# Empty bytes ahead of the tiles that TensorE streams: moving FFN and attention tiles to another byte address

## The chip, the cores and the metric

The kernel runs on one core of a Trainium2 chip. The metric is the device time of one execution in microseconds, the median of several runs. No instruction does other arithmetic after the change than before; what changes is where tiles stand in the core's SBUF (the on-chip memory, 128 partitions wide; an address here is a byte within each partition).

## The reference, cut to what matters

Two layers over 256 latent and 256 context tokens, width 1024, each layer an attention between two SwiGLU FFNs of inner width 2816; layer 0 has differential attention, layer 1 grouped-query attention.

```python
def swiglu(h, w_in, w_out):
    gate, up = jnp.split(h @ w_in, 2, axis=-1)
    return (jax.nn.silu(gate) * up) @ w_out
...
x = x + 0.5 * mod[:, 2] * swiglu(modulate(x, norm_g[i, 0], mod[:, 0], mod[:, 1]), w_ffn_in[i, 0], w_ffn_out[i, 0])
h = modulate(x, norm_g[i, 1], mod[:, 3], mod[:, 4])
y, yc = diff_attention(h, hc, ...)  # layer 0; gqa_attention in layer 1
x = x + mod[:, 5] * y
x = x + 0.5 * mod[:, 8] * swiglu(modulate(x, norm_g[i, 2], mod[:, 6], mod[:, 7]), w_ffn_in[i, 1], w_ffn_out[i, 1])
```

The context stream has the same products with the same weights, up to the last layer, whose last FFN has latent tokens alone.

## The kernel before, in words

**Products.** Activations lie transposed: 128 features on the partitions, the 512 tokens (256 latent, then 256 context) along the free bytes. Every float32 number is split into a rounded part and the rest, `hi` and `lo`, and one product is three matmuls (helper `mac`, lines 384 to 386): `hi` by `hi`, `hi` by the other's `lo`, `lo` by the other's `hi`. The weight, 128 by 128, is held in the array; the activation, 128 by 512 (or 256, or 258), streams past it. Each matmul has its own load of the held tile (PEld), which runs while the matmul before it streams. So while one activation tile streams, the next weight is read too.

**Stages.** In an FFN, half of the inner width at a time (`NH` = 11 tiles): first products `gate` and `up` stream `h_hi`, `h_lo` (24 matmuls each); `gated` makes `a_hi`, `a_lo` of them; the second products `out` stream `a_hi`, `a_lo` (33 matmuls for each of 8 tiles of features). The last two feature tiles of an FFN are done a stream at a time, 256 columns wide, under the name `e`, in `boundary`. The last FFN has 258 (first products) and 256 columns (second products). In the attentions, `qk`, `q`, `k` and `v` stream `h` (in `v` the weight streams and `h` is held), the scores `sps` hold `qs` and stream `ks` and `kl`, and the output projection (`op`) streams `pa`; its second half in layer 0, under the name `e`, streams the first four tiles of `h_hi` and `h_lo`, in which those parts are kept.

**Weights.** `advance` issues each weight's DMA on SP's queue into one of 5 `raw` slots; ScalarE rounds it into one of 6 `whi` slots (line 150), VectorE subtracts into one of 6 `wlo` slots (line 151). The same `raw` slots take the modulation weights (`wm`), which VectorE multiplies and sums (`mod_task`, line 172) between its other work, in program order.

**Where tiles stand.** A pool is laid out when it is opened, tile behind tile in the order in which they are first asked for, each rounded up to 32 bytes, and pools opened later stand behind it. The pools `const`, `wpool`, `stat` and `tmp` stay open for the whole kernel; the FFN's, `da`'s or `gq`'s pool stands behind them, at byte 151072, one after the other in the same place. This gives, with the remainder of the address by 512:

| tiles | part in a product | bytes | remainder before | after |
|---|---|---|---|---|
| `whi`, `wlo` (all 12 slots) | held (in `v` streamed) | 56992 to 106143 | 160 | 160 |
| `hhi0..7`, `hlo0..7` | streamed (in `v` held) | 109728 to 142495 | 160 | 160 |
| `ahi0..10`, `alo0..10` | streamed | from 151072 | 32 | 160 |
| `da`: `kl` / `pa` | streamed | from 151136 | 96 / 96 | 160 / 160 |
| `da`: `ks` / `qs` / `v` | streamed / held / streamed | from 175968 | 352 | 160 |
| `da`: `pe` / `pT` | held | from 213920 | 416 / 160 | 224 / 480 |
| `gq`: `qs`, `ks`, `kl`, `pa`, `v`, `pe` | both | from 151072 | 32 | 160 |
| `gq`: `pT0`, `pT1` | streamed | from 210848 | 416 | 32 |

A tile of 512 float32 columns has 2048 bytes, a held tile 512 bytes, and a weight slot is cut into held tiles at multiples of 512 bytes, so one remainder stands for a whole tile.

Of the kernel before, what the change touches and what calls it, by code (L numbers as in the profile page):

```python
# [11 lines left out]
F32 = mybir.dt.float32  # L12
F32R = mybir.dt.float32r
# [6 lines left out]
P = 128  # L20
D = 1024
KD = D // P
SEQ = 256
CTX = 256
T = SEQ + CTX
# [18 lines left out]
PIECE_AT = (18, 21, 24, 26, 28, 31, 32, 33)  # L44
WARM = 24


@with_exitstack
def trunk(ctx: ExitStack, tc: tile.TileContext, a: dict):
    nc = tc.nc  # L50
    PSUM = bass.MemoryType.PSUM

    const = ctx.enter_context(tc.tile_pool(name="const", bufs=1))
    wpool = ctx.enter_context(tc.tile_pool(name="wpool", bufs=2))
    stat = ctx.enter_context(tc.tile_pool(name="stat", bufs=1))
    tmp = ctx.enter_context(tc.tile_pool(name="tmp", bufs=3))
# [6 lines left out]
    def ax_tile(name):  # L63
        return ax_ps.tile([P, 512], F32, tag="ax", name=name)


    tok = (slice(0, SEQ), slice(SEQ, T))

    sck = tmp.tile([P, KD, 32], F32, tag="sq", name="sck")
# [65 lines left out]
    def raw_tile(name):  # L135
        return wpool.tile([P, 1024], F32, tag="raw", name=name, bufs=5)

    def advance(upto):
        for i in range(len(ready), min(upto, len(flat) - 1) + 1):
            src, pieces, f = flat[i]  # L140
            parts, c0 = [], 0
            for q, kt in enumerate(pieces):
                n = kt * f
                raw = raw_tile(f"raw{i}_{q}")
                nc.sync.dma_start(raw[:, :n], src[:, c0 : c0 + n])
                hi = wpool.tile([P, 1024], F32R, tag="whi", name=f"whi{i}_{q}", bufs=6)
                lo = wpool.tile([P, 1024], F32R, tag="wlo", name=f"wlo{i}_{q}", bufs=6)
                step = n // 2 if i in fine else n
                for c in (slice(b, b + step) for b in range(0, n, step)):
                    nc.scalar.activation(hi[:, c], raw[:, c], AF.Copy)  # L150
                    nc.vector.tensor_tensor(lo[:, c], raw[:, c], hi[:, c].bitcast(F32), op=ALU.subtract)  # L151
                parts += [(hi[:, k * f : k * f + f], lo[:, k * f : k * f + f]) for k in range(kt)]
                c0 += n
            ready[i] = parts

    def weight(i, look=LOOK):
        advance(i + look)
        return ready[i]
# [165 lines left out]
    def table(func, after):  # L324

        t = tmp.tile([P, 1], F32, tag="tab", name="tab")
        return nc.scalar.activation(t, after, func, scale=0.0, bias=1.0)

    h_hi = [stat.tile([P, T], F32R, name=f"hhi{j}", tag=f"hhi{j}") for j in range(KD)]
    h_lo = [stat.tile([P, T], F32R, name=f"hlo{j}", tag=f"hlo{j}") for j in range(KD)]  # L330

    def modulated_tile(l, n3, s, j, rstd, eng=nc.vector):
# [98 lines left out]
    def boundary(groups, nxt, follow):  # L431


        for s in range(2):
            for i, (outs, ends, tiles) in enumerate(groups):
                ps = [mm_tile(f"e{t}") if t < 3 and not (s and i) else ax_tile(f"e{t}") for t in range(tiles)]
                outs(ps, tok[s])
                if s and i == len(groups) - 1:
                    advance(nxt)
                ends(ps, s)  # L440
            if s:
                advance(nxt + 1)
            steps.extend(modulated(*follow, s))
            if s == 0:
                norm_step()
                norm_step()


    def ffn(l, s, n, follow=None, f_steps=0, o_steps=0, upto=(0, 0)):
# [4 lines left out]
        nxt = base  # L454
        with ExitStack() as st:
            fp = st.enter_context(tc.tile_pool(name=f"ffn{l}{s}", bufs=2))
            a_hi = [fp.tile([P, T], F32R, tag=f"ahi{i}", name=f"ahi{i}", bufs=1) for i in range(NH)]
            a_lo = [fp.tile([P, T], F32R, tag=f"alo{i}", name=f"alo{i}", bufs=1) for i in range(NH)]

            def load_sc(after=None):  # L460
# [33 lines left out]
            for hf in range(2):  # L494
                i0 = 0
                if hf == 0 and opening:
                    i0 = G0
                    with tc.tile_pool(name="open", bufs=2) as sp:
# [7 lines left out]
                        for k in range(KD + 2):  # L506
# [8 lines left out]
                            if k > 1:  # L515
                                w = ready[nxt + k - 2]
# [12 lines left out]
                elif hf == 0:  # L529
                    i0 = 2  # L530
                    banks = [mm_tile(f"g{b}") if b < 3 else ax_tile(f"g{b}") for b in range(4)]
                    w = [weight(nxt, 1), weight(nxt + 1, 0)]
# [15 lines left out]
                for i in range(i0, NH):  # L548
                    w = weight(nxt)
# [9 lines left out]
                for jj in range(0, KD, 2):  # L559
# [18 lines left out]
                    w = [weight(nxt), weight(nxt + 1, 0 if final else LOOK)]  # L578
# [97 lines left out]
    def diff_attention(l):  # L676
        base = start["att", l]
        scale = 64 ** -0.5
        with tc.tile_pool(name="da", bufs=2) as ap:
            lam = ap.tile([P, 4], F32, tag="lam", name="lam", bufs=1)  # L680
            nlam = lam[:, 3:4]
            g1 = ap.tile([P, 1], F32, tag="g1", name="g1", bufs=1)

            lamv = tmp.tile([P, 4, 64], F32, tag="ht", name="lamv")
            for i, n in enumerate(("da_lam_q1", "da_lam_k1", "da_lam_q2", "da_lam_k2")):
                nc.scalar.dma_start(lamv[:, i, :], a[n].to_broadcast([P, 64]))

            kls = [[ap.tile([P, T], F32R, tag=f"kl{i}{m}", name=f"kl{i}{m}", bufs=1) for m in range(2)] for i in range(2)]
            for kl in kls:
                zero_others(kl)  # L690

            def lambdas(after):
                lj = ap.tile([P, 64], F32, tag="lj", name="lj", bufs=1)
                for i in range(2):
                    nc.vector.tensor_tensor_reduce(
                        out=lj, in0=lamv[:, 2 * i, :], in1=lamv[:, 2 * i + 1, :], op0=ALU.mult, op1=ALU.add,
                        scale=1.0, scalar=0.0, accum_out=lam[:, i : i + 1],
                    )
                table(AF.Exp, after)
                nc.scalar.activation(lam[:, 0:2], lam[:, 0:2], AF.Exp)  # L700
                nc.vector.tensor_tensor(lam[:, 2:3], lam[:, 1:2], lam[:, 0:1], op=ALU.subtract)
                nc.vector.tensor_scalar(nlam, lam[:, 2:3], -LAM_INIT, None, op0=ALU.add)
                nc.vector.tensor_scalar(g1, subln_g, 1.0 - LAM_INIT, None, op0=ALU.mult)

            pa = [[ap.tile([P, T], F32R, tag=f"pa{i}{k}", name=f"pa{i}{k}", bufs=1) for k in range(4)] for i in range(2)]

            def v_mac(ps, w, k, s_, t):
                c = slice(s_ * 256 + t * P, s_ * 256 + t * P + P)
# [58 lines left out]
            def outputs(hd):  # L767
                ops = ax_tile("ops")
                h = hd["h"]
                for u in range(4):  # L770
                    k0 = 0 if u < 2 else 2
                    for kt in range(k0, 4):
                        nc.tensor.matmul(
                            ops[:, u * P : u * P + P], hd["pT"][u][:, kt - k0, :],
                            hd["v"][:, kt, (h % 2) * P : (h % 2) * P + P], start=kt == k0, stop=kt == 3,
                        )
                o, ms = hd["o"], hd["ms"]
                nc.vector.tensor_copy(o[:, :, h % 2, :], ops.rearrange("p (t f) -> p t f", t=4))
                for u in range(4):
                    osq = ap.tile([P, P], F32, tag="osq", name="osq", bufs=1)  # L780
                    nc.scalar.activation(
                        osq, ops[:, u * P : u * P + P], AF.Square, accum_out=ms[:, u, h % 2 : h % 2 + 1]
                    )
# [26 lines left out]
            def behind(hd, u):  # L810

                turned(hd, u)
                if u == U_AT and done:
                    pair = done.pop()
                    scaled(pair)
                    h = pair["h"]
                    if h < HEADS // 2:
                        parts_of(pair, o_hi[h - 1 : h + 1], o_lo[h - 1 : h + 1])
                    else:
                        late.append(pair)  # L820
                if u == 3:
                    outputs(hd)
                    if hd["h"] % 2:
                        normed(hd)
                        done.append(hd)
# [44 lines left out]
            for s_ in range(2):  # L870
# [5 lines left out]
                for k in range(KD):  # L876
                    for g in range(2):
                        mac(
                            qkps[g][:, tok[s_]], w_part(wqk, k, slice(g * P, g * P + P)), h_part(k, tok[s_]),
                            k == 0, k == KD - 1,  # L880
                        )
            lambdas(last_norm["rstd"][:, 0:1])
            v_tile(0)
            for t in range(2):
# [27 lines left out]
    def gqa(l):  # L912
        base = start["att", l]
        scale = 64 ** -0.5
        with tc.tile_pool(name="gq", bufs=2) as ap:
            qs = [ap.tile([P, SEQ], F32R, tag=f"qs{i % 8}", name=f"qs{i}", bufs=1) for i in range(16)]
            ks = [ap.tile([P, T], F32R, tag=f"ks{i}", name=f"ks{i}", bufs=1) for i in range(4)]
            kl = [ap.tile([P, T], F32R, tag=f"kl{i}", name=f"kl{i}", bufs=1) for i in range(4)]
# [3 lines left out]
            pa = [[ap.tile([P, SEQ], F32R, tag=f"pa{i}{k}", name=f"pa{i}{k}", bufs=1) for k in range(8)] for i in range(2)]  # L922
# [136 lines left out]
            for n, un in enumerate(units + [None, None]):  # L1059
                if un:  # L1060
                    flight.append((un, weights_of(*un)))
                if n in Q_AT:
                    i, g = divmod(Q_AT.index(n), 2)
# [8 lines left out]
                if n in sqs:  # L1072
                    i, sq = sqs[n]
# [11 lines left out]
            out_proj(base + 8, range(4, 8), o_part, l, SEQ, 1, (l, 2))  # L1085

    ffn(0, 0, T, (0, 1), 2, 1, (0, 7))
    diff_attention(0)
    ffn(0, 1, T, (1, 0), 1.5, 1, (1, 1))
    ffn(1, 0, T, (1, 1), 1.5, 1, (1, 8))  # L1090
    gqa(1)
    ffn(1, 1, SEQ)

# [102 lines left out]
```

## Time and profile before

| | |
|---|---|
| median of 3 runs | 1728.6 us (1728.1 to 1730.68) |
| the profiled execution's own time | 1729.97 us |
| its span, first to last instruction | 1727.8 us |
| TensorE (PE) busy | 1707.0 us, 9586 matmuls |
| VectorE (DVE) / ScalarE (ACT) busy | 1159.4 / 730.3 us |
| granted clock, mean | 0.996 |

A matmul's length in the rows runs from its start to its modelled end, and neighbours overlap; what a matmul costs the engine is the distance from its start to the next one's start, here called its pace. It is read from the time order of a stretch without waits: the start of the last row less that of the first, by the number of steps between them.

### The profile page before, as it was taken

Reading aid. Unit: us, or ns where it says so; the run is one execution under the profiler, and the core shown is the slowest. Engines: PE = TensorE matmul, PEld = TensorE weight load, DVE = VectorE, ACT = ScalarE, POOL = GpSimd, SP = SyncE. Lnnn points to the kernel's source line nnn. Section 1 sums busy time; section 2 is a strip of 40 time slices with the busy share of each in tenths; the row PEclk is TensorE's granted clock in tenths of the full one; section 3 lists DMA queues with packets and bytes.
Section 4 is the critical chain, followed back from the end, with each engine's and each line's share of the span. In section 5 each row is a group of like instructions: output and inputs, shape, how many; then the busy total and the mean of one; then the engine's idle time right before and its main releaser. Section 6 shows DMA issues by size and latency. Waiting matters only on the chain.

```text
span 1727.8 us, 24899 instructions
## 1 busy us (share of the span) xinstructions
PE 1707.0 (99%) x9586; PEld 1463.1 (85%) x9586; DVE 1159.4 (67%) x2113; ACT 730.3 (42%) x1359; POOL 26.3 (2%) x42
## 2 busy tenths in 40 slices
PE   9999999999999999999999999999999999999998
PEld 6788888789888889888888898888888897799998
DVE  3697777756888868756766557545543488876664
ACT  3432222235767646322222244222222368765454
POOL 0000000000100000000000000000000010000000
PEclk8999999999999999999999999999999999999999
DMA  7675565442122223545644535546552332145652
GB/s 255 228 242 160 187 215 161 153 151 101 57 67 74 73 74 123 179 140 160 203 156 150 169 110 183 152 132 196 178 160 77 118 101 72 50 164 146 217 162 83
DMA packets 76870, 249.59 MB, mean 144 GB/s; under 512 B 9936, under 2 KB 10064, under 8 KB 76752
## 3 DMA queue, kind: packets, MB, share of 16 engines
q1 hardware_dynamic: 75456, 247.25, 44.9%
q8 instruction: 75, 1.23, 0.3%
q10 hardware_dynamic: 1296, 0.76, 0.1%
q14 instruction: 43, 0.35, 0.1%
HBM read 246.92 MB, written 1.05 MB: 144 GB/s over the span
## 4 chain that ended last, share of the span: by engine, by line
PE 84%; DVE 7%; issue 3%; DMA 2%; ACT 2%; POOL 0%; DVEq 0%; ACTq 0%; POOLq 0%
PE out L385 7%; PE out L386 7%; PE out L384 7%; PE gate L384 7%; PE gate L385 7%; PE gate L386 7%; PE up L385 7%; PE up L386 7%; PE up L384 7%; DMA wm<-in_w_mod 2%; PE g L384 2%; PE g L385 2%; PE g L386 2%; DVE junk L172 1%; PE e L384 1%
## 5 line engine op out<-in xcount | busy, mean ns | idle before, releaser
L150 ACT ACTIVATE whi<-raw 128x1024 fp32r<-128x1024 f32 (+3 forms) x426 | 350.4, 836 | 455.7 <-PE out L385 248.5
L151 DVE TENSOR_TENSOR wlo<-raw,whi 128x1024 fp32r<-128x1024 f32 (+3 forms) x426 | 399.6, 946 | 186.5 <-ACT whi L150 185.7
L172 DVE CUSTOM_DVE_ANT_0 junk<-wm,sc,b_mod 128x1024 bf16<-128x1024 f32 x224 | 287.4, 1283 | 186.4 <-DMA wm<-in_w_mod 182.8
L384 PE MATMUL gate<-hhi,whi 128*128 128x512 f32 (+1 forms) x648 | 234.0, 361 | 0.7 <-DVE av L474 0.7
L386 PE MATMUL gate<-hhi,wlo 128*128 128x512 f32 (+1 forms) x648 | 233.7, 361 | 0.0
L385 PE MATMUL gate<-hlo,whi 128*128 128x512 f32 (+1 forms) x648 | 233.6, 361 | 0.0
L385 PE MATMUL up<-hlo,whi 128*128 128x512 f32 (+1 forms) x648 | 233.6, 361 | 0.0
L384 PE MATMUL up<-hhi,whi 128*128 128x512 f32 (+1 forms) x648 | 233.6, 360 | 0.0
L386 PE MATMUL up<-hhi,wlo 128*128 128x512 f32 (+1 forms) x648 | 233.5, 360 | 0.0
L385 PE MATMUL out<-alo,whi 128*128 128x512 f32 (+1 forms) x638 | 232.3, 364 | 0.0
L384 PE MATMUL out<-ahi,whi 128*128 128x512 f32 (+1 forms) x638 | 232.0, 364 | 0.0
L386 PE MATMUL out<-ahi,wlo 128*128 128x512 f32 (+1 forms) x638 | 231.8, 364 | 0.0
L402 ACT ACTIVATE ahi<-av 128x512 fp32r<-128x512 f32 (+1 forms) x88 | 50.7, 578 | 211.8 <-DVE av L474 204.5
L384 PEld LDWEIGHTS gate<-hhi,whi 128*128 128x128 f32 x648 | 122.4, 189 | 20.2 <-DVE av L474 1.6
L385 PEld LDWEIGHTS out<-alo,whi 128*128 128x128 f32 x638 | 119.9, 188 | 21.4 <-DVE alo L403 0.4
L386 PEld LDWEIGHTS gate<-hhi,wlo 128*128 128x128 f32 x648 | 122.4, 189 | 18.4
L385 PEld LDWEIGHTS up<-hlo,whi 128*128 128x128 f32 x648 | 122.4, 189 | 18.4
L384 PEld LDWEIGHTS up<-hhi,whi 128*128 128x128 f32 x648 | 122.4, 189 | 18.4
L386 PEld LDWEIGHTS up<-hhi,wlo 128*128 128x128 f32 x648 | 122.4, 189 | 18.3
L385 PEld LDWEIGHTS gate<-hlo,whi 128*128 128x128 f32 x648 | 122.4, 189 | 18.2
L386 PEld LDWEIGHTS out<-ahi,wlo 128*128 128x128 f32 x638 | 119.7, 188 | 21.1
L384 PEld LDWEIGHTS out<-ahi,whi 128*128 128x128 f32 x638 | 119.8, 188 | 21.0
(240 smaller groups left out, 2618.0 us busy)
## 6 DMA issues: line engine op xcount, KB each, us to landing
raw<-in_w_in SPq DMA_DIRECT2D x170, 512.0 KB, 4.4
wm<-in_w_mod SPq DMA_DIRECT2D x128, 512.0 KB, 4.2
raw<-in_w_out SPq DMA_DIRECT2D x64, 384.0 KB, 3.4
raw<-in_w_out SPq DMA_DIRECT2D x64, 320.0 KB, 3.1
raw<-in_da_vqk SPq DMA_DIRECT2D x24, 512.0 KB, 3.9
wf<-in_w_mod SPq DMA_DIRECT2D x16, 512.0 KB, 5.0
raw<-in_gq_qkv SPq DMA_DIRECT2D x12, 512.0 KB, 3.8
raw<-in_da_o SPq DMA_DIRECT2D x8, 512.0 KB, 3.7
```

Of the source, the lines that this page charges most:

```text
L150: nc.scalar.activation(hi[:, c], raw[:, c], AF.Copy)
L151: nc.vector.tensor_tensor(lo[:, c], raw[:, c], hi[:, c].bitcast(F32), op=ALU.subtract)
L172: nc.vector.tensor_tensor_reduce(out=junk, in0=raw, in1=mod_pool["sc"][:, s, :], op0=ALU.mult, op1=ALU.add, scale=1.0, scalar=b_mod[:, l, ...
L384: nc.tensor.matmul(out, ah, bh, start=first, stop=False)
L385: nc.tensor.matmul(out, ah, bl, start=False, stop=False)
L386: return nc.tensor.matmul(out, al, bh, start=False, stop=last)
L402: nc.scalar.activation(hi, src, AF.Copy)
```

## The change

Three empty tiles are put ahead of others: 64 bytes ahead of `a_hi` in each FFN's pool, 64 ahead of `kl` in `da`, 64 at the start of `gq`; the other places of the table `GAPS` are 0. `lam` and `g1` (32 bytes each) move from `da` into `tmp`, which pushes everything behind `tmp` by 64 bytes. In `da`, `lj` and `osq` lose their own tiles: `lj` takes the slot of `sw`, `osq` one of the three slots `sq` of `tmp`. The number and kind of the instructions of each engine stay.

```diff
+GAPS = dict(const=0, w=0, norm=(0, 0), ffn=(64, 0), da=(64, 0), gq=64)
...
+    def gap(pool, i, n):
+
+        if n:
+            pool.tile([P, n // 4], F32, tag=f"gap{i}", name=f"gap{i}", bufs=1)
+
...
+    lam = tmp.tile([P, 4], F32, tag="lam", name="lam", bufs=1)
+    nlam = lam[:, 3:4]
+    g1 = tmp.tile([P, 1], F32, tag="g1", name="g1", bufs=1)
+
+    gap(stat, 0, GAPS["norm"][0])
     h_hi = [stat.tile([P, T], F32R, name=f"hhi{j}", tag=f"hhi{j}") for j in range(KD)]
+    gap(stat, 1, GAPS["norm"][1])
...
             fp = st.enter_context(tc.tile_pool(name=f"ffn{l}{s}", bufs=2))
+            gap(fp, 0, GAPS["ffn"][0])
             a_hi = [fp.tile([P, T], F32R, tag=f"ahi{i}", name=f"ahi{i}", bufs=1) for i in range(NH)]
+            gap(fp, 1, GAPS["ffn"][1])
...
-            lam = ap.tile([P, 4], F32, tag="lam", name="lam", bufs=1)
-            nlam = lam[:, 3:4]
-            g1 = ap.tile([P, 1], F32, tag="g1", name="g1", bufs=1)
...
+            gap(ap, 0, GAPS["da"][0])
...
-                lj = ap.tile([P, 64], F32, tag="lj", name="lj", bufs=1)
+                lj = ap.tile([P, 1, SEQ], F32, tag="sw", name="lj", bufs=1)[:, 0, 0:64]
...
-                    osq = ap.tile([P, P], F32, tag="osq", name="osq", bufs=1)
+                    osq = tmp.tile([P, 256], F32, tag="sq", name="osq")[:, 0:P]
...
         with tc.tile_pool(name="gq", bufs=2) as ap:
+            gap(ap, 0, GAPS["gq"])
```

## Rows read from the trace of the kernel before

**Rows 1.** The page's part 1 (busy time of each engine), the granted clock of part 2 in 40 slices, and part 4 (the chain that ended last, by engine).

```profile
PE 1707.0 (99%) x9586; PEld 1463.1 (85%) x9586; DVE 1159.4 (67%) x2113; ACT 730.3 (42%) x1359; POOL 26.3 (2%) x42
...
PEclk8999999999999999999999999999999999999999
...
PE 84%; DVE 7%; issue 3%; DMA 2%; ACT 2%; POOL 0%; DVEq 0%; ACTq 0%; POOLq 0%
```

**Rows 2.** Busy time by stretch (from:to in us, its length, then busy us and number of instructions of PE, PEld, DVE, ACT and POOL, the granted clock, the DMA share, GB/s). First and third row: two stretches of the FFNs' second products. Second and fourth: the stretch of first products right behind each.

```profile
160.80:222.00 61.20, 61.20 (x264) 49.22 (x263) 44.29 (x69) 14.39 (x17) 0.00 (x0) 1.00 0.59 187
222.50:283.50 61.00, 61.00 (x271) 50.52 (x270) 45.10 (x66) 16.54 (x20) 0.00 (x0) 1.00 0.61 197
...
1147.00:1208.10 61.10, 61.10 (x263) 49.18 (x262) 33.32 (x50) 14.35 (x17) 0.00 (x0) 1.00 0.61 186
1208.60:1269.60 61.00, 61.00 (x271) 50.52 (x270) 31.03 (x42) 17.94 (x22) 0.00 (x0) 1.00 0.57 181
```

**Rows 3.** Groups of TensorE's matmuls by line and shape, whole span: number, busy us, mean ns of one, idle time of the engine before them and what ended it.

```profile
L384 PE MATMUL gate<-hhi,whi 128*128 128x512 f32 x472 | 184.1, 390 | 0.7 <-DVE av L474 0.7
...
L386 PE MATMUL out<-ahi,wlo 128*128 128x512 f32 x462 | 182.5, 395 | 0.0
...
L385 PE MATMUL out<-alo,whi 128*128 128x256 f32 x176 | 49.8, 283 | 0.0
...
L384 PE MATMUL e<-ahi,whi 128*128 128x256 f32 x132 | 37.7, 285 | 0.0
...
L630 PE MATMUL sps<-ks,qs 128*128 128x512 f32 x64 | 28.9, 452 | 3.3 <-ACT ks L625 3.1 <-ACT pe L1023 0.2
...
L384 PE MATMUL op<-pa,whi 128*128 128x256 f32 x64 | 18.8, 296 | 1.0 <-ACT pe L1023 1.0
...
L384 PE MATMUL op<-pa,whi 128*128 128x512 f32 x32 | 12.8, 401 | 0.0
```

**Rows 4.** Time order of TensorE in the first products (gate and up) of the third FFN's second half: start, length in us. The first and the last of 197 rows in a row, one matmul each.

```profile
1208.37 0.39 PE L384 MATMUL gate<-hhi,whi 128*128 128x512 f32 x1
...
1252.81 0.39 PE L385 MATMUL gate<-hlo,whi 128*128 128x512 f32 x1
```

**Rows 5.** The same in the second products (out) of the third FFN's first half: the first and the last of 197 rows in a row, one matmul each.

```profile
1146.78 0.40 PE L384 MATMUL out<-ahi,whi 128*128 128x512 f32 x1
...
1192.51 0.40 PE L385 MATMUL out<-alo,whi 128*128 128x512 f32 x1
```

**Rows 6.** The same across a border: the first and last of 29 rows of the first FFN's second products, then the first and last of the 32 rows of first products behind them.

```profile
215.43 0.39 PE L385 MATMUL out<-alo,whi 128*128 128x512 f32 x1
...
221.96 0.39 PE L386 MATMUL out<-ahi,wlo 128*128 128x512 f32 x1
222.19 0.39 PE L384 MATMUL gate<-hhi,whi 128*128 128x512 f32 x1
...
229.23 0.39 PE L385 MATMUL up<-hlo,whi 128*128 128x512 f32 x1
```

**Rows 7.** The same in the first layer's output projection, whose streamed tiles are `pa`: the first and the last of 47 rows.

```profile
620.12 0.40 PE L385 MATMUL op<-pa,whi 128*128 128x512 f32 x1
...
630.86 0.40 PE L386 MATMUL op<-pa,wlo 128*128 128x512 f32 x1
```

**Rows 8.** The same in the part of that projection whose streamed tiles are `h_hi` and `h_lo`, 256 columns wide: the first and the last of 112 rows.

```profile
632.09 0.28 PE L385 MATMUL e<-hlo,whi 128*128 128x256 f32 x1
...
645.40 0.28 PE L385 MATMUL e<-hlo,whi 128*128 128x256 f32 x1
```

**Rows 9.** The same in the last FFN's second products, 256 columns wide: the first and the last of 177 rows.

```profile
1600.96 0.28 PE L386 MATMUL out<-ahi,wlo 128*128 128x256 f32 x1
...
1621.84 0.28 PE L385 MATMUL out<-alo,whi 128*128 128x256 f32 x1
```

**Rows 10.** The page's part 5, the conversion of weights: ScalarE's `whi` and VectorE's `wlo`, with the idle time of the engine before them and what ended most of it.

```profile
L150 ACT ACTIVATE whi<-raw 128x1024 fp32r<-128x1024 f32 (+3 forms) x426 | 350.4, 836 | 455.7 <-PE out L385 248.5
L151 DVE TENSOR_TENSOR wlo<-raw,whi 128x1024 fp32r<-128x1024 f32 (+3 forms) x426 | 399.6, 946 | 186.5 <-ACT whi L150 185.7
```

**Rows 11.** The chain that ended last, 204 to 224 us: start, length, what.

```profile
206.72 0.25 PE out L386
...
206.99 0.04 DVE x L407
...
214.11 4.64 DMA wm<-in_w_mod
```

**Rows 12.** Time order of VectorE there; in brackets the idle time before the instruction and what ended it.

```profile
206.99 0.88 DVE L407 SCALAR_TENSOR_TENSOR x<-out,mod,x 128x256 f32<-128x256 f32 x2 [1.28 <-PE out L386]
...
218.88 1.28 DVE L172 CUSTOM_DVE_ANT_0 junk<-wm,sc,b_mod 128x1024 bf16<-128x1024 f32 x1 [1.68 <-DMA wm<-in_w_mod]
```

**Rows 13.** Time order of TensorE, 305 to 313 us: the one row with an idle time before it.

```profile
310.16 0.50 PE L384 MATMUL gate<-hhi,whi 128*128 128x512 f32 x1 [0.75 <-DVE av L474]
```

**Rows 14.** Busy time by stretch, columns as in rows 2: first the differential attention of layer 0, then the grouped one of layer 1.

```profile
397.50:655.00 257.50, 251.03 (x1639) 225.19 (x1639) 206.49 (x478) 166.51 (x424) 15.24 (x20) 1.00 0.21 71
1383.00:1530.00 147.00, 144.00 (x1048) 122.01 (x1047) 126.50 (x346) 111.92 (x253) 9.88 (x10) 1.00 0.24 77
```

More of the change, by code (lines that the diff above doesn't have):

```diff
@@ L64, in ax_tile @@
         return ax_ps.tile([P, 512], F32, tag="ax", name=name)
+    gap(const, 0, GAPS["const"])
     tok = (slice(0, SEQ), slice(SEQ, T))
@@ L146, in advance @@
                 hi = wpool.tile([P, 1024], F32R, tag="whi", name=f"whi{i}_{q}", bufs=6)
+                if i == q == 0:
+                    gap(wpool, 0, GAPS["w"])
                 lo = wpool.tile([P, 1024], F32R, tag="wlo", name=f"wlo{i}_{q}", bufs=6)
@@ L703, in lambdas @@
                 nc.vector.tensor_scalar(g1, subln_g, 1.0 - LAM_INIT, None, op0=ALU.mult)
-            pa = [[ap.tile([P, T], F32R, tag=f"pa{i}{k}", name=f"pa{i}{k}", bufs=1) for k in range(4)] for i in range(2)]
+            pa = []
+            for i in range(2):
+                if i:
+                    gap(ap, 1, GAPS["da"][1])
+                pa.append([ap.tile([P, T], F32R, tag=f"pa{i}{k}", name=f"pa{i}{k}", bufs=1) for k in range(4)])
             def v_mac(ps, w, k, s_, t):
```

## The prediction

> **What bounds the kernel now.** I read four views, in this order. The page first: TensorE is busy 99% of the span, at full granted clock in all slices but the first, and it carries 84% of the chain that ended last [rows 1]. So the time is, to first order, the sum of TensorE's paces, and the question is what one matmul costs. The stretches come second. The reader is to compare two kinds that stand side by side: in 61.1 us of second products 263 matmuls start, in 61.0 us of first products behind them 271 [rows 2]. Both have TensorE busy all the time, both have 512 columns, and the clock is 1.00 in both. Third, the groups: a first product is 389 to 390 ns long, a second product 395, without idle time before it apart from one 0.7 us [rows 3]. Fourth, the time order, which gives the paces: 196 steps of first products take 1252.81 - 1208.37 = 44.44 us, that is 226.7 ns each [rows 4]; 196 steps of second products take 1192.51 - 1146.78 = 45.73 us, that is 233.3 ns each [rows 5]. The pace changes at the border itself: 28 steps before it at 6.53 / 28 = 233.2 ns, 31 behind it at 7.04 / 31 = 227.1 [rows 6].
>
> Both kinds hold weights of remainder 160. First products stream `h`, remainder 160; second products stream `a`, remainder 32. The output projection of layer 0 streams `pa`, remainder 96: its pace is 10.74 / 46 = 233.5 ns [rows 7]. So in three groups of 512 columns the one in which streamed and held tile have the same remainder is 6.6 to 6.8 ns faster than the two in which they differ. That is the trace's own trial of the change, though not a clean one: see the first rival.
>
> With 256 columns it goes the other way. The layer-0 projection's part that streams `h` (160) has 13.31 / 111 = 119.9 ns [rows 8], the last FFN's second products, which stream `a` (32), 20.88 / 176 = 118.6 ns [rows 9].
>
> **The change part by part.**
>
> *FFN second products, 512 columns.* `mac` issues three matmuls a step, and each of its lines has 462 of them [rows 3]: 3 x 462 = 1386. After the change they have the remainders of the first products. I take their pace: 1386 x (233.3 - 226.7) = 9.15 us less. Bounds: 0 if the remainder is not what sets the pace, 9.15 if it is; I take 9.15, since the first products are the nearest row in everything but held layout and length of the sum (24 against 33 matmuls).
>
> *Output projection of layer 0, 512 columns.* 3 x 32 = 96 matmuls [rows 3]. 48 stand in the dense stretch of rows 7: 48 x 6.8 = 0.33 us less. The other 48 stand between the scores, where TensorE is idle 6.5 us of 257.5 [rows 14], so there the gain may go into waits: between 0 and 0.33 us. I take 0.3 for all.
>
> *Scores.* 64 + 64 matmuls of 512 columns whose `ks`, `kl` go to 160. Their mean is 452 ns with waits before them [rows 3], so no pace can be read. Between 0 and 128 x 6.8 = 0.9 us less; I take 0, as the attentions' stretches are the ones with idle time [rows 14].
>
> *Products of 256 columns that stream `a` or `pa`.* 3 x 176 in the last FFN, 3 x 132 under `e`, 3 x 64 in layer 1's projection [rows 3]: 1116. Taking the pace of rows 8 for that of rows 9 costs 1116 x 1.3 = 1.45 us more. Below, nothing; I take the 1.45, for the same reason as the 9.15.
>
> *`pT`, `pe` and the layer-1 `v`.* The words of the change say all tiles; by the layout `pT` goes to 480 and 32, `pe` in `da` to 224. In these products, 128 columns or two passes, I take nothing; they stand in the stretches with idle time [rows 14].
>
> *`lam`, `g1`, `lj`, `osq`, the gaps.* No instruction is added. `lj` and `sw` are both written by VectorE, `osq` by ScalarE alone into slots whose readers finished in the FFN before: no new wait with anything queued behind it. Nothing, hidden by program order; if one came, it would be a wait of one engine once per head.
>
> *What the faster TensorE triggers.* Weights are no limit: ScalarE is idle 455.7 us before its conversions, 248.5 of them because a second product has not yet freed the slot [rows 10]; conversions wait for TensorE. There is one place where something else is late. From 206.72 us, the chain leaves TensorE for VectorE and the modulation weights' DMAs, 4.64 us the first of them [rows 11], and it comes back at 310.16 us, where TensorE waits 0.75 us for `av` [rows 13]. This chain starts when a pair of second products ends: there VectorE had been idle 1.28 us [rows 12]. By then (46 us at 233.3 ns) 198 matmuls have gained 6.6 ns each, 1.3 us, and the chain starts that much earlier. The whole stretch has 264 matmuls [rows 2] and gains 1.74 us. The difference, 0.44 us, is given back as a longer wait at 310 us; if the DMAs do not move up at all, 1.74. I take 0.5.
>
> Sum: -9.15 - 0.3 + 1.45 + 0.5 = -7.5 us. The profiled execution took 1729.97 us, 2.2 more than its span of 1727.8; the span would become 1720.3, the execution 1722.5. The median of the runs shown lies 1.4 below that execution, so the median is forecast at 1721.1 us.
>
> **The rivals.**
>
> *The remainder is not the cause.* Every slow group also lies higher in SBUF (from 151072) than every fast one (up to 142495), `out` sums 33 matmuls where `gate` sums 24, and its held tiles are 512 bytes apart where those of `gate` are 1024. Any of these could make the 6.6 ns, and none is changed. For it: scores with the same remainder on both sides show no clear gain. Against it: `pa` and `a` differ in held layout and in the length of the sum (12 and 33 matmuls) and have almost one pace [rows 5, 7]. Then nothing moves, or the 256-column loss alone: 1728.6 to 1730. Two rules of the Trainium skill stand on this side. "TensorE: Matmul & The Clock Gate", Part 2, says that the engine has two independent read ports, one for the streamed and one for the held operand, so that loading the next weights takes nothing from the running matmul; by it the sum would be 0 and the time 1728.6. "SBUF — State Buffer", Door 1, gives lines of 16 bytes as what counts for full rate; 32, 96 and 160 are all whole lines, so again 0. The paces of rows 4 and 5 differ where these rules make no difference, so I give them little.
>
> *Matching costs wide products what it costs narrow ones (slower).* Rows 8 and 9 say that the same remainder is 1.3 ns worse for 256 columns. If that is the remainder's real effect, and the 6.6 ns belong to something else, 512 columns lose 2.6 ns: 1386 x 2.6 + 1.45 = 5.1 us more, 1733.7. It decides once a wide matmul loses 1.5 ns (2.05 us over 1386, with the 1.45 more than 3.5 us). Against it: rows 6, where pace falls within the same microsecond as the remainder changes.
>
> *The gain is eaten by VectorE.* The give-back at 310 us grows and repeats in the second FFN, whose VectorE also does modulation work. Against it: over the whole span the first products waited only once [rows 3]. Half the gain lost: about 1725.
>
> **How the numbers follow.** The forecast has 0.85; VectorE eating half 0.04; the remainder not the cause 0.08; slower 0.03. About 0.2% (3.5 us) is what a measurement of this kernel can tell from no change: faster 0.89, same 0.08, slower 0.03. The forecast's own range: all bounds low, -9.15 - 0.65 - 0.9 = -10.7, 1717.9; all bounds high, -9.15 + 1.45 + 1.74 = -6.0, 1722.6. The runs shown reach 2 us above their median, so I give 1718 to 1724; it leaves out the 0.15 of the rivals.
>
> **What would show it.** In the profile after: second products of 512 columns at a pace near 226.7 ns and a mean length near 389 instead of 395; first products unchanged; the last FFN's second products near 119.9 ns; `op` with 512 columns near 227; the wait for `av` in the first FFN at 1 to 2.5 us instead of 0.7. The prediction is wrong if `out` stays at 233 ns, or if it falls and the span does not.

## Result and profile after

The changed kernel takes 1719.3 us at the median of six runs (1718.06 to 1721.13), beside 1728.87 us for the kernel before on the same chip: ratio 0.9944 [0.9932, 0.9957], 9.6 us less. The profiled execution of after took 1718.06 us with a span of 1715.9 us. It is the fastest of its six, while the profiled execution of before lay 1.1 us above its median; so the two profiles differ by 11.9 us and the medians by 9.6.

The page of after: busy time, granted clock, and the chain that ended last (answers [rows 1]).

```profile
PE 1696.9 (99%) x9586; PEld 1464.5 (85%) x9586; DVE 1159.3 (68%) x2113; ACT 729.3 (43%) x1359; POOL 26.1 (2%) x42
...
PEclk8999999999999999999999999999999999999999
...
PE 86%; DVE 5%; issue 3%; ACT 3%; DMA 2%; POOL 0%; DVEq 0%; ACTq 0%; POOLq 0%
```

TensorE has lost 10.1 us of busy time with the same 9586 matmuls, at the same clock. Its groups by line and shape, columns as in [rows 3]:

```profile
L400 PE MATMUL gate<-hhi,whi 128*128 128x512 f32 x472 | 184.0, 390 | 0.1
...
L402 PE MATMUL out<-ahi,wlo 128*128 128x512 f32 x462 | 179.8, 389 | 0.0
...
L401 PE MATMUL out<-alo,whi 128*128 128x256 f32 x176 | 50.0, 284 | 0.0
...
L400 PE MATMUL e<-ahi,whi 128*128 128x256 f32 x132 | 37.8, 287 | 0.0
...
L648 PE MATMUL sps<-ks,qs 128*128 128x512 f32 x64 | 28.9, 452 | 2.5 <-ACT ks L643 2.2 <-ACT pe L1044 0.2
```

A second product is now 389 ns long, as a first product is, where it was 395; the 256-wide ones are 1 to 2 ns longer; the scores have the length that they had. The time order of TensorE in after, first and last row: 199 rows of the third FFN's second products (answers [rows 5]), then 47 rows of layer 0's output projection (answers [rows 7]).

```profile
1137.42 0.39 PE L400 MATMUL out<-ahi,whi 128*128 128x512 f32 x1
...
1182.30 0.39 PE L400 MATMUL out<-ahi,whi 128*128 128x512 f32 x1
...
613.27 0.40 PE L401 MATMUL op<-pa,whi 128*128 128x512 f32 x1
...
623.75 0.39 PE L402 MATMUL op<-pa,wlo 128*128 128x512 f32 x1
```

Paces: 44.88 / 198 = 226.7 ns (233.3 before) and 10.48 / 46 = 227.8 ns (233.5 before).

Where the 11.9 us of the two profiles lie, stage by stage (from the first matmul of a stage to the first of the next):

| stage | before, us | after, us | difference |
|---|---|---|---|
| second products with 512 columns, 3 FFNs | 3 x (61.59 + 46.19) | 3 x (59.84 + 44.88) | -9.18 |
| the same, 256 columns (end of 3 FFNs; last FFN) | 3 x 17.28; 31.60, 34.89 | 3 x 17.42; 31.91, 35.14 | +0.98 |
| layer 0's attention with its projection | 225.19 | 222.60 | -2.60 |
| last FFN, first products, second half | 63.35 | 63.80 | +0.45 |
| first FFN, first products (two halves) | 87.21, 121.03 | 87.15, 120.37 | -0.72 |
| opening | 72.33 | 71.45 | -0.88 |

The rest adds 0.05. The opening took 71.45 to 73.47 us in the 14 kernels profiled here and follows no edit; it is not counted as an effect.

### The profile page after: what moved, and what is told of

Read it like the earlier page. It is cut to its first block, busy times and chain, and to the rows that moved or that the text cites. A ratio compares the mean times of both kernels' runs of the same rounds, so it can differ in the third digit from the quotient of the medians.

```text
span 1715.9 us, 24904 instructions
## 1 busy us (share of the span) xinstructions
PE 1696.9 (99%) x9586; PEld 1464.5 (85%) x9586; DVE 1159.3 (68%) x2113; ACT 729.3 (43%) x1359; POOL 26.1 (2%) x42
## 4 chain that ended last, share of the span: by engine, by line
PE 86%; DVE 5%; issue 3%; ACT 3%; DMA 2%; POOL 0%; DVEq 0%; ACTq 0%; POOLq 0%
PE out L401 7%; PE out L402 7%; PE out L400 7%; PE gate L400 7%; PE gate L402 7%; PE up L400 7%; PE gate L401 7%; PE up L401 7%; PE up L402 7%; DMA wm<-in_w_mod 2%; PE g L400 2%; PE g L401 2%; PE g L402 2%; DVE junk L182 1%; PE qk L401 1%
## 5 line engine op out<-in xcount | busy, mean ns | idle before, releaser
L402 PE MATMUL up<-hhi,wlo 128*128 128x512 f32 (+1 forms) x648 | 233.5, 360 | 0.0
L400 PE MATMUL up<-hhi,whi 128*128 128x512 f32 (+1 forms) x648 | 233.5, 360 | 0.0
```

The costliest lines, as they stand in the source:

```text
L400: nc.tensor.matmul(out, ah, bh, start=first, stop=False)
L402: return nc.tensor.matmul(out, al, bh, start=False, stop=last)
```

## Experiments

Distance below means the streamed operand's byte address less the held one's, modulo 512. Paces in the tables are means, start to start, over the steps of a kind that follow each other without a break; the few steps of over 130 ns at 256 or 258 columns, or over 250 at 512, which hold a wait or something in between, are left out. In all these runs the tiles of a kind that are held share one remainder, so the runs can't tell the held tile in use from the one that is loaded meanwhile.

### Which part of the change carries the gain

`ffn_only`: the kernel before, with one edit.

```diff
+            fp.tile([P, 32], F32, tag="gap", name="gap", bufs=1)
             a_hi = [fp.tile([P, T], F32R, tag=f"ahi{i}", name=f"ahi{i}", bufs=1) for i in range(NH)]
```

> The kernel before with one edit: 128 empty bytes ahead of the FFNs' a tiles, so that they go from remainder 32 to 160; the attentions' tiles stay where they were. If the remainder sets the pace of the 512-column products, out goes from 233.3 to 226.7 ns: 1386 x 6.6 = 9.1 us less, and the 924 products of 256 columns that stream a cost 1.0 to 1.2 us more: about 8 us less than before, near 1721. The attention of layer 0, which was 2.6 us shorter in the changed kernel, then takes as long as before. If the attention's shortening follows from the FFN or from chance, it shows here too.

`osq_only`: the kernel before, with one other edit.

```diff
-                    osq = ap.tile([P, P], F32, tag="osq", name="osq", bufs=1)
+                    osq = tmp.tile([P, 256], F32, tag="sq", name="osq")[:, 0:P]
```

> The kernel before with one edit: osq takes the three slots sq of tmp instead of its own single slot; no streamed or held tile moves. If the 2.6 us that layer 0's attention lost come from ScalarE no longer writing one slot over and over, they appear here: 1726.3, and the jumps of 0.4 to 0.9 us behind osq. If they come from the remainders of kl, ks, qs, pa, nothing changes: 1728.9.

`ffn_only` took 1721.87 us against 1729.13 (ratio 0.9956 [0.9943, 0.9968]), with the second products at 226.7 ns and layer 0's attention at 225.21 us, as before. Time order of TensorE in `ffn_only`, first and last of 193 rows of the third FFN's second products:

```profile
1142.24 0.39 PE L384 MATMUL out<-ahi,whi 128*128 128x512 f32 x1
...
1185.76 0.39 PE L384 MATMUL out<-ahi,whi 128*128 128x512 f32 x1
```

43.52 / 192 = 226.7 ns, where before had 233.3 [rows 5]. `osq_only` took 1728.31 us (0.9992 [0.9984, 1.0001]): no difference by its time, but its trace has the attention at 223.04 us, 2.15 less, and the second products at 233.3 ns. So the 2.3 us that the prediction did not have in the attention (2.6 less the 0.3 of the output projection) come mostly from `osq`, and not from a remainder; this rests on profiles of the stage, since the time of the whole kernel can't show it.

How: compared instruction by instruction, `ffn_only` has exactly the order of before on TensorE, VectorE and ScalarE. `osq_only` and the changed kernel differ from it on TensorE in the same places of this attention, three in all. With one slot, a head's four squares are strung out between the exponentials; with the `sq` slots they stand together. Time order of ScalarE, third and fourth square of one head, first `ffn_only`, then `osq_only`:

```profile
484.41 0.28 ACT L782 ACTIVATE osq<-ops 128x128 f32<-128x128 f32 x1
...
484.66 0.70 ACT L747 ACTIVATE pe<-sps,mx 128x512 f32<-128x512 f32 x1
...
485.32 0.29 ACT L782 ACTIVATE osq<-ops 128x128 f32<-128x128 f32 x1
```

```profile
485.96 0.28 ACT L781 ACTIVATE osq<-ops 128x128 f32<-128x128 f32 x1
...
486.21 0.28 ACT L781 ACTIVATE osq<-ops 128x128 f32<-128x128 f32 x1
...
486.46 0.70 ACT L746 ACTIVATE pe<-sps,mx 128x512 f32<-128x512 f32 x1
```

A little later, time order of TensorE, `ffn_only` and then `osq_only`:

```profile
488.14 0.60 PE L763 MATMUL tps<-ident,pe 128*128 128x128 f32 x4
488.50 0.48 PE L384 MATMUL qk<-hhi,whi 128*128 128x512 f32 x1
...
489.58 1.23 PE L804 MATMUL otps<-ident,o 128*128 128x128 f32 x8
...
491.13 0.39 PE L384 MATMUL qk<-hhi,whi 128*128 128x512 f32 x1
```

```profile
490.51 0.60 PE L762 MATMUL tps<-ident,pe 128*128 128x128 f32 x4
490.94 1.04 PE L803 MATMUL otps<-ident,o 128*128 128x128 f32 x8
...
492.29 0.39 PE L384 MATMUL qk<-hhi,whi 128*128 128x512 f32 x1
```

In the old order three `qk` matmuls stand between the two groups of transposes. From `tps` to the next `qk` step behind the scores it takes 2.99 us with these three (0.68 us at 226.7 ns), 1.78 without: 0.53 us lost at this one place. The same happens once more at 540 us; the third place is in the output projection. The old order gave 225.19 and 225.21 us for this stage in the two kernels that have it, 222.36 to 224.17 came in the twelve with the `sq` slots. That the slot's release sets the order is the likeliest reason, since nothing else was edited in `osq_only`; how the order is arrived at no trace shows.

### Is it the remainder 160, or that both sides agree?

`all_224`: the changed kernel, everything 64 bytes further on.

```diff
-GAPS = dict(const=0, w=0, norm=(0, 0), ffn=(64, 0), da=(64, 0), gq=64)
+GAPS = dict(const=64, w=0, norm=(0, 0), ffn=(64, 0), da=(64, 0), gq=64)
```

> The changed kernel with 64 more empty bytes at the very start: weights, h, a and the attentions' tiles all go from 160 to 224, so streamed and held still have the same remainder. If only the match counts, all paces stay (226.7 and 119.9 ns) and the time is that of the changed kernel, 1719.3. If 160 itself counts, gate, up and out all slow by 2.2 to 6.6 ns: 4218 products of 512 columns x 6.6 = 28 us more, up to 1747.

1720.36 us, ratio 0.9944 [0.9932, 0.9957], the ratio of the changed kernel, and the paces stay at 226.7 and 119.9 ns. First and last of 195 rows of its third FFN's second products, 43.97 / 194 = 226.7 ns:

```profile
1138.29 0.39 PE L400 MATMUL out<-ahi,whi 128*128 128x512 f32 x1
...
1182.26 0.39 PE L402 MATMUL out<-ahi,wlo 128*128 128x512 f32 x1
```

Both sides moved by 64 bytes change nothing: what counts is not the remainder 160.

`h_224`: `h` alone moved, which turns the mismatch onto the first products.

```diff
-GAPS = dict(const=0, w=0, norm=(0, 0), ffn=(64, 0), da=(64, 0), gq=64)
+GAPS = dict(const=0, w=0, norm=(64, 0), ffn=(0, 0), da=(0, 0), gq=0)
```

> The changed kernel with 64 empty bytes ahead of h_hi and h_lo instead of ahead of the FFNs' and attentions' tiles: h is at 224, weights, a and the attentions' tiles stay at 160. If the match counts, first products (gate, up, 2832 of 512 columns), qk, k and g slow from 226.7 to 233 to 234 ns, some 3300 x 6.6 = 22 us more: 1741; the 258-column products of the last FFN get 1 to 1.3 ns faster each (1056: 1.3 us), so 1739 to 1741. If higher place or the kind of product counts, nothing changes: 1719.

Time order of TensorE in `h_224`, first and last of 197 rows of the third FFN's first products:

```profile
1205.09 0.39 PE L401 MATMUL gate<-hlo,whi 128*128 128x512 f32 x1
...
1249.95 0.39 PE L402 MATMUL gate<-hhi,wlo 128*128 128x512 f32 x1
```

44.86 / 196 = 228.9 ns: slower than 226.7, as agreement wants, but by 2.2 ns and not 6.6, and the 256-wide products that stream or hold `h` became faster (`v` 119.8 to 115.6 ns in the mean, `e` with `h` 119.9 to 116.2). The kernel took 1721.77 us (0.9954 [0.9939, 0.9969]), far below what was expected. A mismatch has no single price.

### The price by distance

`a_sweep_1`, `a_sweep_2`, `a_sweep_3`: the changed kernel with another gap ahead of `a` in each FFN, so that `a` lies at 224, 288, 416 and 256; at 0, 352, 480 and 320; at 128, 192, 64 and 448 (first to last FFN). For the first:

```diff
-            gap(fp, 0, GAPS["ffn"][0])
+            gap(fp, 0, {(0, 0): 128, (0, 1): 192, (1, 0): 320, (1, 1): 160}[l, s])
```

> The changed kernel with the a tiles of the four FFNs at four places: remainder 224, 288, 416 and 256 (weights stay at 160, so 64, 128, 256 and 96 bytes ahead). Read per FFN: the pace of out. If any mismatch costs the same, the 512-column ones have 233 ns in all three FFNs. If the distance counts, as the 229 ns of the run with h at 224 says, 224 gives 229 and the others lie between 227 and 235. If the period were 256 bytes, 416 would give 226.7.

> The same at remainder 0, 352, 480 and 320 (352, 192, 320 and 160 bytes ahead of the weights' 160). If the distance counts, the paces of the three 512-column FFNs differ; if any mismatch costs the same, 233 ns in all. The 256-column products (e in the first three, out in the last) go between 115 and 120 ns.

> The same at remainder 128, 192, 64 and 448 (32 behind, 32 ahead, 96 behind, 224 behind the weights' 160). If the loss grows with the distance, 128 and 192 lie nearest to 226.7 and 64 is above 233; if only the exact match locks, all three have 229 to 234.

They took 1722.03, 1723.62 and 1729.16 us (single runs, beside 1730.72 of before). Time order of TensorE in `a_sweep_1`, first and last of 192, 188 and 185 rows of second products: `a` at 224, 288 and 416.

```profile
170.12 0.39 PE L400 MATMUL out<-ahi,whi 128*128 128x512 f32 x1
...
213.83 0.39 PE L402 MATMUL out<-ahi,wlo 128*128 128x512 f32 x1
...
783.16 0.40 PE L400 MATMUL out<-ahi,whi 128*128 128x512 f32 x1
...
826.80 0.39 PE L401 MATMUL out<-alo,whi 128*128 128x512 f32 x1
...
1148.18 0.39 PE L400 MATMUL out<-ahi,whi 128*128 128x512 f32 x1
...
1189.88 0.39 PE L401 MATMUL out<-alo,whi 128*128 128x512 f32 x1
```

43.71 / 191 = 228.8, 43.64 / 187 = 233.4 and 41.70 / 184 = 226.6 ns. At 416 the operands differ by 256 bytes, and the pace is that of agreement. All that was measured, folded at 256 (in brackets the distances modulo 512):

| distance mod 256 | 512 columns, ns | 256 columns, ns |
|---|---|---|
| 0 | 226.7 (0, 256) | 119.8 to 119.9 (0, 256) |
| 32 | 233.3 (32) | 116.8, 117.2 (32, 288) |
| 64 | 229.0 (64, 320) | 117.8, 116.2 (64, 320) |
| 96 | 233.4 (352) | 119.9 (96, 352) |
| 128 | 233.3 (128, 384) | 118.6 (128, 384) |
| 160 | 234.3 (416) | 118.3, 117.5 (160, 416) |
| 192 | 233.3, 233.5 (192, 448) | 113.3 to 117.8 (192, 448) |
| 224 | 233.3 (480) | 118.3 (480) |

At 512 columns the four pairs that lie 256 bytes apart (0 and 256, 64 and 320, 128 and 384, 192 and 448) agree within 0.2 ns, so what counts repeats after 256 bytes; only 0 is fast and 64 is close. For narrow products 0 and 96 are the slowest and 192 is the fastest, by 2 to 7 ns.

Narrow products have no single pace at a distance. In `h_224` every `v` stands at 448. Time order of TensorE, first and last of 48 rows each, two `v` of layer 0 that follow each other:

```profile
470.63 0.28 PE L400 MATMUL v<-whi,hhi 128*128 128x256 f32 x1
...
475.96 0.28 PE L402 MATMUL v<-whi,hlo 128*128 128x256 f32 x1
...
495.85 0.28 PE L400 MATMUL v<-whi,hhi 128*128 128x256 f32 x1
...
501.38 0.28 PE L402 MATMUL v<-whi,hlo 128*128 128x256 f32 x1
```

5.33 / 47 = 113.4 and 5.53 / 47 = 117.7 ns, and the three behind them go on in turn (113.4, 117.8, 113.3). No operand's remainder differs between them; what chooses the pace is not shown.

`a_lo_224`: `a_hi` at 160, `a_lo` at 224, so that two of `mac`'s three lines agree.

```diff
-GAPS = dict(const=0, w=0, norm=(0, 0), ffn=(64, 0), da=(64, 0), gq=64)
+GAPS = dict(const=0, w=0, norm=(0, 0), ffn=(64, 64), da=(64, 0), gq=64)
```

> The changed kernel with 64 bytes between a_hi and a_lo: a_hi stays at 160, a_lo goes to 224, so one matmul in three is mismatched. If each matmul pays for itself, two of the three lines of out stay at 226.7 and the third has 229, mean 227.5. If the loss hangs on the whole sequence, all three lines change.

First and last of 172 rows of its third FFN's second products:

```profile
1150.10 0.40 PE L400 MATMUL out<-ahi,whi 128*128 128x512 f32 x1
...
1189.77 0.39 PE L400 MATMUL out<-ahi,whi 128*128 128x512 f32 x1
```

39.67 / 171 = 232.0 ns (1723.76 us in one run). From their start to the next start the two lines that agree take 231.2 and 232.6 ns, the one that doesn't 232.2: worse for all three than a distance of 64 in all three (229.0). So the price is not one of the single matmul; it hangs on the sequence. Single steps say the same: where operands agree each step takes 226 or 227 ns, at distance 384 in the kernel before the steps alternate between 229 and 238.

### Versions that use it

`last_a_352` puts the last FFN's `a`, whose products are 256 wide, at distance 192. The other three build on it: `last_a_h_352` streams the last FFN's `h` (258 columns) from 192 further on as well, by placing it at columns 48 to 305 of its tiles; `last_all_352` adds 192 bytes ahead of layer 1's `pa`; `last_h_224` is that with `h` 16 columns on, distance 64.

```diff
-            gap(fp, 0, GAPS["ffn"][0])
+            gap(fp, 0, 256 if n == SEQ else GAPS["ffn"][0])
...
     WIDE = SEQ + 2
+    OFF = 48
+    ON = slice(OFF, OFF + SEQ)
...
-        nc.scalar.activation(h_hi[j][:, :SEQ], x[j][:, :SEQ], AF.Copy, scale=g)
+        nc.scalar.activation(h_hi[j][:, ON], x[j][:, :SEQ], AF.Copy, scale=g)
...
+            gap(ap, 1, 192)
             pa = [[ap.tile([P, SEQ], F32R, tag=f"pa{i}{k}", name=f"pa{i}{k}", bufs=1) for k in range(8)] for i in range(2)]
```

> The changed kernel, with the last FFN's a moved from byte 160 to byte 352 modulo 512 (192 away from the held weights); its products there are 256 wide. If narrow products run best 192 bytes from their held operand, as other 256-wide products did in the sweep of a (113.5 to 114.8 ns against 119.9 matched), its 528 output products go from 119.7 to about 114 ns: -2.6 to -3.3 us, 1716.0 to 1716.7 us at the median. If the sweep's gain belonged to the half-wide products at an FFN's end alone, 119 ns as before and 1719.3 us. If matching is best at each width, as the prediction had it for wide ones, slower than 1719.3.

> The kernel of last_a_352, and in the last FFN h lies 48 columns (192 bytes) further on within its tiles, so that its 1056 gate and up products of 258 columns also stream from byte 352 against weights held at 160. Measured so far at that width: 120.0 to 120.45 ns at distance 0, 118.9 at 64. If 192 is best here too, about 115 ns: another -4.7 to -5.8 us, 1710.5 to 1712 us at the median. If the two columns more than 256 break the rule, 119 to 121 ns and within 1 us of last_a_352.

> The kernel of last_a_h_352, and the second attention's pa at byte 352 as well: its 192 output products of 256 columns go from 119.7 to about 114.5 ns, -1.0 us against last_a_h_352 (1709.5 to 1711 us), if nothing else ends later; if the attention's work around them sets their time, no difference.

> The kernel of last_all_352 with the last FFN's h 16 columns (64 bytes) further on instead of 48: its 1056 gate and up products of 258 columns stream from byte 224 against 160. At that distance this width took 118.9 ns when all of h lay there, against 120.0 matched and 120.9 at 192: -2.1 us against last_all_352, 1714.3 to 1715.3 us at the median. If the price hangs on the phase at which the sequence starts and not on the distance, 120 to 121 ns and 1716 to 1717.5 us.

| kernel | median, us | ratio to before | 258 columns, ns | last `out`, ns | `op` 256, ns |
|---|---|---|---|---|---|
| after | 1719.3 | 0.9944 [0.9932, 0.9957] | 120.0 and 120.8 (two halves) | 119.9 | 119.7 |
| `last_a_352` | 1716.74 | 0.9928 [0.9916, 0.9941] | 120.0 | 114.0 and 114.8 (two halves) | 119.7 |
| `last_a_h_352` | 1717.32 | 0.9931 [0.9918, 0.9945] | 120.8 | 113.6 | 119.7 |
| `last_all_352` | 1716.91 | 0.9929 [0.9916, 0.9941] | 120.8 | 113.5 | 117.0 |
| `last_h_224` | 1714.21 | 0.9918 [0.9904, 0.9932] | 119.0 | 113.5 | 114.5 |

Time order of TensorE in `last_a_352`, first and last of 123 rows of the last FFN's second products (answers [rows 9]):

```profile
1592.08 0.28 PE L402 MATMUL out<-ahi,wlo 128*128 128x256 f32 x1
...
1605.90 0.28 PE L401 MATMUL out<-alo,whi 128*128 128x256 f32 x1
```

13.82 / 122 = 113.3 ns, where before had 118.6 and after 119.9. The narrow rule holds there. It does not hold with 258 columns, where `last_a_h_352` was expected to give 115 ns: at 192 both halves take 120.8 ns, which after has in its second half at distance 0 too, and only 64 gains (119.0). So two columns more are enough to change the best distance. The `op` of `last_all_352` and `last_h_224` stands at the same distance in both, 192, and has 117.0 and 114.5 ns: one more case of two paces. `last_h_224` is the best kernel of this study: span 1711.6 us against 1715.9 of the changed one, and intervals that only touch (0.9932). Its interval overlaps that of `last_a_352`, so the last 2.5 us are likely and not certain; the other two gave nothing that can be measured on top of `last_a_352`.

## Why the prediction was right

Direction and range held: 1721.1 forecast (1718 to 1724), 1719.3 measured; -7.5 us against -9.6. By its terms:

- *Second products, -9.15:* right to 0.03 us (-9.18). The step "I take their pace" was exact. Its reason was right in kind and too coarse: not the same remainder modulo 512 but a distance of 0 modulo 256, and another distance need not cost 6.6 ns. Before lay at 384, one of the dear ones; the trace of before had no cheap one to show. The rule that the prediction weighed from the Trainium skill, "TensorE: Matmul & The Clock Gate", Part 2, on two independent read ports, would give nothing here and does not account for the trace's 6.6 ns a matmul; whether reading the next weight is what costs them, no run here shows.
- *Output projection of layer 0, -0.3:* the pace came as forecast (227.8 ns); its 0.3 us lie in a stage that moved for another reason.
- *Scores, 0:* 452 ns before and after. The prediction could have had this from its own table of places: in layer 0 `ks` stood 0 and `kl` 256 bytes from the held `qs`, in layer 1 both stood at 0, which by the sweep is agreement already. So there was nothing to gain, and the scores were no evidence for the first rival.
- *256 columns, +1.45:* +0.98 on the path. The pace went to 119.9 as taken; layer 1's projection (0.25 of the sum) stands among the attention's work, whose stage got 0.13 longer, and at an FFN's end the change was 0.14 over 132 such products, 1.1 ns each.
- *`osq`: "Nothing, hidden by program order".* This step failed: -2.60 us in the stage, -2.15 of them with `osq` alone. The prediction looked for a new wait and found none; what it did not ask is whether fewer slots had shaped the order in which the engines' work was laid out. It had the right row, idle time in that stage [rows 14], and used it as cover only.
- *VectorE's give-back, +0.5, shown by a wait of 1 to 2.5 us:* did not come. Chain and TensorE's time order in after, at the two ends of that stretch (answers [rows 11, 13]):

```profile
204.75 0.04 DVE x L423
```

```profile
306.85 0.50 PE L400 MATMUL gate<-hhi,whi 128*128 128x512 f32 x1
```

  From `x` on VectorE to that matmul it takes 102.1 us, before 103.2 (206.99 to 310.16): the chain got 1.1 us shorter, TensorE's 66 second products inside it 0.44, and the rest went out of the wait. The step onto this matmul is 0.53 us, where before has 1.14. It is no steady effect: the same step took 1.50 in `osq_only`, 0.71 in `ffn_only`, 1.12 in `all_224`, 0.39 in `last_h_224`, and in four others no step there is over 0.28. Between two profiles this place moves by 1 us for reasons that the runs here do not settle.
- *Not in the sum:* +0.45 us in the last FFN's first products of 258 columns, whose operands did not move. In after's second half their steps run through a cycle of eight (121, 113, 122, 120, 120, 123, 125 and 122 ns, within 1), in `last_a_352` and in the first half they stand at 120. It comes from the change, through the second products just ahead: `ffn_only` moved `a` alone and has the same 63.80 us, `last_a_352` moved the last FFN's `a` from 0 to 192 and is back at 63.35. Of the ten kernels that stream this `h` at 0, the six with that `a` at 0, 32 or 96 modulo 256 (in one of them `a_lo` at 64) have 63.79 or 63.80, the four at 128, 160 or 192 have 63.35 or 63.36. So a sequence keeps a rhythm that it falls into, and the products ahead of it matter; why, stays open.

Of the rivals, "the remainder is not the cause" fell with `ffn_only` and `all_224`; "matching costs wide products" fell with rows of after at 226.7 ns, though its premise (narrow products lose by matching) is true. From profile to profile the forecast was short by 4.4 us (-7.5 against -11.9): 2.3 in the attention, 1.2 at 310 us, 0.9 in the opening, 0.5 in the narrow products, less 0.45 in the 258-wide ones. At the median it was short by 1.8 only: it put the median 1.4 us below a profiled execution, as in before, and after's lies 1.2 above. So the main term was right for its reason, and that the total at the median came so near is in part luck: the misses at `osq` and at 310 us are partly hidden by where the profiled executions happened to lie among their runs.

## What to carry to other kernels

Where TensorE is busy all the time, compare the start-to-start paces of matmuls of one shape before looking for idle time: 6.6 ns on 1386 of them were 9 us here with no wait in any view. Then try the distance between streamed and held tiles for each width on the chip, since here the 512-wide products wanted 0 modulo 256 and the 256-wide ones 192, and neither follows from the other. And look at scratch tiles with a single slot in a stage with idle time: more slots, with nothing else edited, changed the order of the other engines.

## What the runs showed of the hardware

- The pace of a 512-column matmul of this type runs from 226.7 ns at distance 0 to 234.3 at 416 with nothing else edited than where tiles stand, and repeats after 256 bytes of distance. Operands that agree have the same pace at remainder 160 and at 224.
- The pace of a 256-column one runs from 113.3 to 120.0 ns. The distance does not settle it alone: at 192 modulo 256 it was 113.3 to 114.8 in some stretches and 117.0 to 117.8 in others.
- The effect belongs to a sequence: one operand in three at another distance slowed all three lines (226.7 to 232.0 ns), and products of 258 columns took 120.0 or 120.8 ns as the `a` of the products ahead of them was moved.
- Two columns decide: at distance 192 a product of 256 columns goes from 119.9 to 113.3 ns, one of 258 stays at 120.8, and gains 1 at 64.
